# First two projection sections by turns: four accumulators fed by row blocks instead of two sections one after the other

## The chip, the cores and the metric

The kernel runs on one core of a Trainium2 chip. The core has a matrix engine (TensorE, PE in the profile), a vector engine (VectorE, DVE), an activation engine (ScalarE, ACT), GpSimd (POOL), and SyncE (SP), which here only issues DMAs; ACT issues some DMAs too. The metric is the device time of one execution in microseconds (us), as the median of several runs. The time before is 370.73 us (three runs, 370.17 to 373.01).

## The reference

One decoder layer for 256 tokens of width 1024, all in float32. What matters here is its front: the RMS norm of x, one wide input projection, and the small network that compresses keys and values.

```python
h = rmsnorm(x, norm1_g[layer])
proj = h @ w_in[layer]
q_n = proj[..., :OFF_KV]
kv_n = proj[..., OFF_KV:OFF_GN]
g_n = proj[..., OFF_GN:OFF_M]
...
k_c, v_c, k_s, v_s, k_w, v_w = (kv[:, :, i] for i in range(6))
k_s = partial_rope(k_s, cos, sin)
k_w = partial_rope(k_w, cos, sin)
kc = compress_blocks(k_c, cmp_pe_k[layer], cmp_k_w1[layer], cmp_k_w2[layer])
vc = compress_blocks(v_c, cmp_pe_v[layer], cmp_v_w1[layer], cmp_v_w2[layer])

def compress_blocks(k, pe, w1, w2):
    ...
    return jax.nn.gelu(kb @ w1) @ w2
```

Behind it come two attentions (a sparse one with 8 heads in 2 groups, and one with 8 heads), gates, an output projection, and a feed-forward part of width 4096 with a squared ReLU. The change touches only the first two sections of the projection and the steps that hang on them.

## The kernel before

**Weights in chunks.** All weights are streamed through three buffers `raw` as chunks of 128 partitions by up to 2048 numbers (`CHUNKS`, numbered from 0). Each matrix product is made exact by three products of rounded parts: `split` rounds a chunk to `whi` on ACT (L114) and leaves the rest, `wlo`, on DVE (L116); `mm3` multiplies high by high, high by low and low by high. `whi` and `wlo` have three buffers each as well, so the split of a chunk waits until PE is done with the chunk three tiles earlier, and the load of a chunk waits until the splits of the chunk three tiles earlier are done.

**The projection.** Chunks 0 and 1 are the section "kva" (384 columns: keys and values to compress, and the selected-block keys), 2 and 3 "kvb" (408 columns), 4 and 5 "q" (512), 6 and 7 "qm", and so on. The first chunk of a section holds the input rows 0 to 511 of the weights, as four row blocks of 128, the second chunk rows 512 to 1023. `xstat` makes the 24 matmul instructions of one chunk: two accumulators (token tiles t = 0, 1), four row blocks, three products. In chunks 0 and 1 the order goes by row block, with both accumulators in each, and in later chunks by accumulator. The transposed input xT arrives in parts (`x_part`), and a row block kt of it is scaled by the norm's gain and split to `hTh` (ACT, L187) and `hTl` (DVE, L193).

**Who sets the order.** Each engine executes its instructions in the order of the program text. `at(pos, f, ...)` books a step of other work into a chunk's run of matmuls, and `run_slot` emits it ahead of the matmul at that fraction of the run. So the text sets PE's order by position, and the order on ACT, DVE and SP by the sequence of the bookings. A DMA on SP or ACT that must wait for a buffer stops all that stands behind it on that engine's queue. A DMA also takes one of eight semaphore lanes in turn, and its issue waits until the DMA eight places earlier has landed.

**The steps the change moves.** `row_squares`, `row_sums`, `row_norm` compute the rows' norm (rstd). `evac_tm("kva", ...)` scales the two kva accumulators by it into `kcd` (L304) and `kva` (L307) on ACT. `cmp_gather` transposes `kcd` on PE (eight transposes, L372), `gather_evac` adds the position term into `kE` on DVE (eight adds, L384). `cmp_mlp1` is the first layer of the compressing network: 32 small matmuls of `kE` with `w1`, evacuated to `raw1` on ACT (L395), and on DVE a reduction `gsum` (L396). `cmp_sum` multiplies `raw1` by `gsum` on PE and runs the GELU; `cmp_mlp2` is the second layer. `transp_k` transposes the rotated keys. `gate_evac` puts the branch gates through a tanh on ACT (L424) and a scaling on DVE (L426).

## Time and profile before

| | |
|---|---|
| median of three runs | 370.73 us |
| the profiled execution | 371.17 us, of which its span 369.4 us |
| PE busy | 360.8 us (98%) |
| DVE, ACT busy | 311.6 us (84%), 234.2 us (63%) |
| HBM read, written | 64.87 MB, 1.05 MB |
| first matmul of the projection | starts at 4.50 us |
| first matmul of section q | starts at 25.85 us |
| first matmul of section qm | starts at 39.73 us |

All times in the rows are counted from the span's start; the profiled execution is 1.77 us longer than its span. A row of the timeline gives start, length, engine, line and operation with its tiles; the length of a matmul includes its way through the pipeline, so the distance from one start to the next tells its cost. "whi<-raw x2" are two like instructions in one row. A DMA row gives size and the time from issue to landing.

### The profile page before, as it was taken

To read this page: it belongs to the slowest core of one execution; us is meant where nothing else is said; L and a number is where in the kernel's file an instruction comes from. 1 tells how busy PE (TensorE), PEld (TensorE's weight loads), DVE (VectorE), ACT (ScalarE), POOL (GpSimd) and SP (SyncE) were. 2 spreads that over 40 slices of the span, in tenths; PEclk is the share of its full clock that TensorE was granted. 3 is DMA by queue.
4 is the path that set the end of the run, shared out by engine and by line. 5 is a ranking of instruction groups with operands and counts; after the bars stand their busy time and mean duration, and the time that the engine had idled before them with its cause. 6 is when DMAs were issued, how large, how long until landed. Compare 5 with 4: busy or idle time off the path is not lost.

```text
span 369.4 us, 5952 instructions
## 1 busy us (share of the span) xinstructions
PE 360.8 (98%) x2387; PEld 318.5 (86%) x2387; DVE 311.6 (84%) x454; ACT 234.2 (63%) x353; POOL 3.7 (1%) x15
## 2 busy tenths in 40 slices
PE   8999999999999999999999999999999999999993
PEld 6987778877778888788999999999999999999983
DVE  4988879896967769766878999999999999995875
ACT  5984364757747667525465888876766677764522
POOL 1010000000000000000000000000000000000000
PEclk9999999999999999999999999999999999999999
DMA  8987436333533334533583655444565566544003
GB/s 265 398 317 295 138 111 227 114 115 114 172 148 137 115 114 137 206 115 114 178 333 119 229 227 220 171 185 184 184 213 215 227 230 227 221 177 174 0 0 114
DMA packets 11402, 66.28 MB, mean 179 GB/s; under 512 B 1264, under 2 KB 3056, under 8 KB 4080
## 3 DMA queue, kind: packets, MB, share of 16 engines
q1 hardware_dynamic: 10512, 64.55, 47.5%
q10 hardware_dynamic: 864, 1.38, 1.1%
q8 instruction: 18, 0.29, 0.3%
q14 instruction: 8, 0.07, 0.0%
HBM read 64.87 MB, written 1.05 MB: 178 GB/s over the span
## 4 chain that ended last, share of the span: by engine, by line
PE 93%; DMA 1%; ACT 1%; issue 1%; DVE 1%; SPq 0%; POOLq 0%; POOL 0%; DVEq 0%
PE acc L238 62%; PE o L238 10%; PE yb L238 6%; PE tp L238 4%; PE qacc L238 3%; PE kvbacc L238 2%; PE Sa L238 2%; PE Sa L556 1%; DMA gx<-in_gx_dram 1%; PE tp L327 1%; PE Sb L556 1%; ACT whi L114 1%; PE Sb L238 1%; PE o L843 0%; DVE wlo L116 0%
## 5 line engine op out<-in xcount | busy, mean ns | idle before, releaser
L116 DVE TENSOR_TENSOR wlo<-raw,whi 128x1024 fp32r<-128x1024 f32 (+3 forms) x85 | 109.8, 1310 | 11.2 <-ACT whi L114 11.1
L114 ACT ACTIVATE whi<-raw 128x1024 fp32r<-128x1024 f32 (+3 forms) x84 | 93.2, 1138 | 32.1 <-PE acc L238 21.8
L238 PE MATMUL acc<-h2h,whi 128*128 128x256 f32 x256 | 70.9, 277 | 0.0
L238 PE MATMUL acc<-h2l,whi 128*128 128x256 f32 x256 | 70.7, 276 | 0.0
L238 PE MATMUL acc<-h2h,wlo 128*128 128x256 f32 x256 | 70.7, 276 | 0.0
L238 PE MATMUL acc<-whi,hTh 128*128 128x512 f32 (+1 forms) x128 | 50.7, 396 | 0.3 <-ACT whi L114 0.3
L238 PE MATMUL acc<-wlo,hTh 128*128 128x512 f32 (+1 forms) x128 | 50.5, 394 | 0.1
L238 PE MATMUL acc<-whi,hTl 128*128 128x512 f32 (+1 forms) x128 | 49.4, 386 | 0.0
L238 PEld LDWEIGHTS acc<-h2l,whi 128*128 128x128 f32 x256 | 48.1, 188 | 0.0
L238 PEld LDWEIGHTS acc<-h2h,whi 128*128 128x128 f32 x256 | 48.1, 188 | 0.0
L238 PEld LDWEIGHTS acc<-h2h,wlo 128*128 128x128 f32 x256 | 48.1, 188 | 0.0
L949 ACT ACTIVATE whi<-wt 128x2048 fp32r<-128x2048 f32 x13 | 25.0, 1921 | 25.3 <-PE acc L238 24.2
L238 PEld LDWEIGHTS acc<-whi,hTh 128*128 128x128 f32 x128 | 24.3, 190 | 6.7 <-issue 1.3
L951 DVE TENSOR_TENSOR wlo<-wt,whi 128x2048 fp32r<-128x2048 f32 x13 | 29.7, 2285 | 0.1
L238 PEld LDWEIGHTS acc<-wlo,hTh 128*128 128x128 f32 x128 | 24.2, 189 | 4.6 <-DVE wlo L116 0.7
L238 PEld LDWEIGHTS acc<-whi,hTl 128*128 128x128 f32 x128 | 24.2, 189 | 4.5
L942 DVE TENSOR_TENSOR sl<-raw,sh 128x1536 fp32r<-128x1536 f32 x13 | 22.8, 1752 | 0.0
L940 ACT ACTIVATE sh<-raw 128x1536 fp32r<-128x1536 f32 x13 | 19.4, 1489 | 3.0 <-PE acc L238 3.0
L238 PE MATMUL acc<-mxl,whi 128*128 128x256 f32 x64 | 17.8, 278 | 0.0
L238 PE MATMUL acc<-mxh,wlo 128*128 128x256 f32 x64 | 17.8, 278 | 0.0
L238 PE MATMUL acc<-mxh,whi 128*128 128x256 f32 x64 | 17.7, 276 | 0.0
L901 DVE TENSOR_TENSOR al<-aq,ah 128x896 fp32r<-128x896 f32 (+1 forms) x16 | 16.2, 1011 | 0.6 <-ACT ah L899 0.6
(279 smaller groups left out, 732.7 us busy)
## 6 DMA issues: line engine op xcount, KB each, us to landing
raw<-in_ff_dram SPq DMA_DIRECT2D x32, 1024.0 KB, 4.9
raw<-in_gm_dram SPq DMA_DIRECT2D x8, 1024.0 KB, 4.8
raw<-in_wout_dram SPq DMA_DIRECT2D x4, 1024.0 KB, 4.9
raw<-in_q_dram SPq DMA_DIRECT2D x2, 1024.0 KB, 7.1
raw<-in_qm_dram SPq DMA_DIRECT2D x2, 1024.0 KB, 6.1
raw<-in_km_dram SPq DMA_DIRECT2D x2, 1024.0 KB, 5.4
raw<-in_vm_dram SPq DMA_DIRECT2D x2, 1024.0 KB, 4.8
raw<-in_upn_dram SPq DMA_DIRECT2D x2, 1024.0 KB, 5.6
```

The source lines that it names most:

```text
L114: act.activation(hi[c][:, a:b], raw[c][:, a:b], AF.Copy)
L116: dve.tensor_tensor(lo[c][:, a:b], raw[c][:, a:b], hi[c][:, a:b].bitcast(F32), op=ALU.subtract)
L238: pe.matmul(o, l, r, start=start, stop=stop, skip_group_check=True)
L327: pe.transpose(tp[:, j * 256 + t * 128:j * 256 + t * 128 + 128], src[:, t, (2 * i + j) * 128:(2 * i + j + 1) * 128], ident)
L556: pe.transpose(T[:, j, x, o:o + 128], P[:, 2 * x + j, c:c + 128], ident)
L901: dve.tensor_tensor(A[i][2][:, 0:b - a], aq[:, a:b], A[i][1][:, 0:b - a].bitcast(F32), op=ALU.subtract)
L940: act.activation(singles[c][0], v, AF.Copy)
L942: dve.tensor_tensor(singles[c][1], v, singles[c][0].bitcast(F32), op=ALU.subtract)
L949: act.activation(hi[c], v, AF.Copy)
L951: dve.tensor_tensor(lo[c], v, hi[c].bitcast(F32), op=ALU.subtract)
```

## The change

The two sections kva and kvb are no longer computed one after the other. Their chunks are loaded in quarters by turns (0 and 2 by row block, then 1, then 3), and PE goes through the rows once: for each row block of x first six matmuls of kva, then six of kvb, in four accumulators. Chunk order of the buffers is now 0, 2, 1, 3, 4, 5. Chunk 3 is loaded by two DMAs that ACT issues. `sm` and `kc` are loaded after all quarters, and `load(5)`, `load(6)` and w1 are booked behind them at the end of the first run. The evacuations of kva (`kcd_evac` for both tiles, then `kva_evac`) come at the end of the second run; `cmp_gather` stands in chunk 4 instead of 3, `cmp_mlp1` in chunk 5 at 0.08 instead of chunk 4 at 0.7, `cmp_sum` in chunk 5 at 0.4 instead of 0.09, and `cmp_mlp2` with the second `transp_k` in chunk 6 at 0.02 instead of chunk 5 at 0.75. What is computed is the same.

```diff
--- before.py
+++ after.py
@@ -131,22 +132,26 @@
     w1 = ap_.tile([128, 2, 16, 64], F32, name="w1", tag="w1")
     xsq = ap_.tile([128, 8, 256], F32, name="xsq", tag="early")
     gx = cp.tile([128, 16 + 2048], F32, name="gx")
-    raw_tile(0)
-    raw_tile(1)
+    for c in (0, 2, 1):
+        raw_tile(c)
 
     def x_part(a, b):
         c0, c1 = (16 + 256 * a if a else 0), 16 + 256 * b
         nc.sync.dma_start(gx[:, c0:c1], gxd[:, c0:c1])
 
-    for k in range(3):
-        load_part(0, k, 4, 1, nc.scalar)
-    for a, b in ((0, 1), (1, 2), (2, 4)):
-        x_part(a, b)
-    load_part(0, 3, 4)
-    for a in (4, 6):
-        x_part(a, a + 2)
-        load_part(1, a % 4, 4, 2)
-    load(2)
+    load_part(0, 0, 4, 1, nc.scalar)
+    load_part(2, 0, 4, 1, nc.scalar)
+    load_part(0, 1, 4, 1, nc.scalar)
+    x_part(0, 1)
+    x_part(1, 2)
+    load_part(2, 1, 4)
+    for k in (2, 3):
+        x_part(k, k + 1)
+        load_part(0, k, 4)
+        load_part(2, k, 4)
+    for k in (4, 6):
+        x_part(k, k + 2)
+        load_part(1, k % 4, 4, 2)
 
     make_identity(nc, ident)
     dve.memset(mhalf, -0.5)
@@ -159,10 +164,6 @@
     pool.memset(bdk[:, 30:32], 0.0)
 
     xT = gx[:, 16:].rearrange("p (k q) -> p k q", k=8)
-    load(3)
-    nc.sync.dma_start(sm, small)
-    nc.sync.dma_start(kc_, const)
-    load(4)
     g1, g2 = gx[:, 0:8], gx[:, 8:16]
     pe_sb = sm[:, S_PE:S_PE + 32].rearrange("p (s l) -> p s l", s=2)
     w2 = sm[:, S_W2:S_W2 + 128]
@@ -183,7 +184,7 @@
 
     hTh, hTl = act_pair("hT", 16)
 
-    for kt in range(8):
+    def x_block(kt):
         act.activation(hTh[:, kt, :], xT[:, kt, :], AF.Copy, scale=g1[:, kt:kt + 1])
         if kt == 0:
             hi[0] = wp.tile([128, 2048], F32R, name="whi")
@@ -194,6 +195,12 @@
                                  hTh[:, kt, :].bitcast(F32), op0=ALU.mult, op1=ALU.subtract)
         if kt:
             split(kt // 4, kt % 4, 4)
+
+    for kt in range(4):
+        x_block(kt)
+        split(2, kt, 4)
+    nc.sync.dma_start(sm, small)
+    nc.sync.dma_start(kc_, const)
 
     stat = cp.tile([128, 8], F32, name="stat")
     rstd = cp.tile([128, 2], F32, name="rstd")
@@ -253,7 +260,7 @@
         r = []
         h, l = hi[c], lo[c]
         order = [(t, k) for t in range(2) for k in range(4)]
-        if c < 2:
+        if c < 4:
             order.sort(key=lambda e: e[1])
         for t, k in order:
             kt = kts[k]
@@ -297,13 +304,16 @@
     kcd = ap_.tile([128, 2, 4, 2, 64], F32, name="kcd")
     kvb = ap_.tile([128, 2, 408], F32, name="kvb")
     vm = ap_.tile([128, 2, 512], F32, name="vm")
-    tm = {"kva": kva, "kvb": kvb, "vm": vm}
+    tm = {"kvb": kvb, "vm": vm}
+
+    def kcd_evac(t, acc):
+        act.activation(kcd[:, t], acc[:, 0:256].rearrange("p (a d) -> p a d", a=4)[:, :, None, :]
+                       .to_broadcast([128, 4, 2, 64]), AF.Copy, scale=rstd[:, t:t + 1])
+
+    def kva_evac(t, acc):
+        act.activation(kva[:, t, :], acc[:, 256:384], AF.Copy, scale=rstd[:, t:t + 1])
 
     def evac_tm(sec, t, acc, n):
-        if sec == "kva":
-            act.activation(kcd[:, t], acc[:, 0:256].rearrange("p (a d) -> p a d", a=4)[:, :, None, :]
-                           .to_broadcast([128, 4, 2, 64]), AF.Copy, scale=rstd[:, t:t + 1])
-            acc, n = acc[:, 256:384], 128
         act.activation(tm[sec][:, t, :], acc[:, :n], AF.Copy, scale=rstd[:, t:t + 1])
 
     def rope(z, nh):
@@ -605,73 +615,82 @@
             at(0.12, d_yevac, d - 1)
 
 
-    groups = [("kva", 0, 384), ("kvb", C_KVB, 408), ("q", C_Q, 512), ("qm", C_QM, 512),
-              ("km", C_KM, 512), ("vm", C_VM, 512)]
+    first = [acc_tile(), acc_tile()]
+    second = [ps_e.tile([128, 512], F32, name=f"kvbacc{t}") for t in range(2)]
+    x_block(4)
+    raw_tile(3)
+    for k in (0, 2):
+        load_part(3, k, 4, 2, nc.scalar)
+    load(4)
+    row_squares(0)
+    row_squares(1)
+    for i in range(2):
+        a = xstat(i, 384, first, range(4 * i, 4 * i + 4))
+        if i == 0:
+            b = xstat(2, 408, second, range(4))
+
+            at(0.9, x_block, 5)
+            at(0.9, split, 3, 0, 4)
+            at(0.9, row_sums, 0, 2, 2)
+            at(0.9, split, 3, 1, 4)
+            at(0.9, row_squares, 2)
+            at(0.9, x_block, 6)
+            at(0.9, row_squares, 3)
+            for q in ((4, 6, 2), (0, 4, 2), (0, 1, 1)):
+                at(0.9, row_sums, *q)
+            at(0.9, split, 3, 2, 4)
+            at(0.9, x_block, 7)
+            at(0.9, split, 3, 3, 4)
+            at(0.95, load, 5)
+            at(0.95, load, 6)
+            at(0.95, nc.sync.dma_start, w1, w1c)
+        else:
+            b = xstat(3, 408, second, range(4, 8))
+            at(0.58, row_norm)
+            for k in range(2):
+                at(0.6, split, 4, k, 2)
+            at(0.61, load, 7)
+            for t in range(2):
+                at(0.9, kcd_evac, t, first[t])
+            for t in range(2):
+                at(0.91, kva_evac, t, first[t])
+            for k in range(2):
+                at(0.95, split, 5, k, 2, "h")
+        run_slot([m for k in range(0, 24, 6) for x in (a, b) for m in x[k:k + 6]])
+
+    groups = [("q", C_Q, 512), ("qm", C_QM, 512), ("km", C_KM, 512), ("vm", C_VM, 512)]
     for sec, c0, n in groups:
         if sec in ("q", "qm", "km"):
             tm[sec] = ap_.tile([128, 2, 512], F32, name="qtm", bufs=2)
-        if sec in ("kvb", "q"):
+        if sec == "q":
             accs = [ps_e.tile([128, 512], F32, name=f"{sec}acc{t}") for t in range(2)]
         else:
             accs = [acc_tile(), acc_tile()]
         for i in range(2):
             c = c0 + i
-            if c == 0:
-                at(0.6, load, 5)
-            elif c == 1:
-                at(0.88, row_squares, 0)
-                for k in range(4):
-                    at(0.89, split, 2, k, 4)
-                for k in range(1, 4):
-                    at(1.1, row_squares, k)
-                at(1.1, row_sums, 0, 2, 2)
-                at(1.1, row_sums, 4, 6, 2)
-                at(1.1, row_sums, 0, 4, 2)
-                at(1.1, row_sums, 0, 1, 1)
-                for k in range(4):
-                    at(1.2, split, 3, k, 4, "h")
-                for k in range(2):
-                    at(1.3, split, 3, k, 4, "l")
-
-            elif c == 2:
-                at(0.9, row_norm)
-                for k in range(2, 4):
-                    at(0.91, split, 3, k, 4, "l")
-                at(0.92, load, 6)
-                at(0.92, nc.sync.dma_start, w1, w1c)
-            elif c == 3:
-                for k in range(2):
-                    at(0.0, split, 4, k, 2, "h")
-                for t in range(2):
-                    at(0.01, evac_tm, "kva", t, first[t], 384)
-                for k in range(2):
-                    at(0.1, split, 4, k, 2, "l")
-                at(0.11, load, 7)
-                at(0.66, cmp_gather)
-                for k in range(2):
-                    at(0.66, gather_evac, k)
-                for k in range(2):
-                    at(0.7, split, 5, k, 2, "h")
-            elif c == 4:
+            if c == 4:
                 for t in range(2):
                     at(0.0, evac_tm, "kvb", t, second[t], 408)
-                at(0.1, split, 5, 0, 2, "l")
+                at(0.1, cmp_gather)
+                at(0.1, gather_evac, 0)
+                at(0.12, split, 5, 0, 2, "l")
+                at(0.13, gather_evac, 1)
                 at(0.2, rope, kva, 2)
                 at(0.3, split, 5, 1, 2, "l")
                 at(0.35, load, 8)
                 split_events(c, (0.5, 0.55), (0.8, 0.9))
-                at(0.7, cmp_mlp1)
             else:
                 std_events(c)
             unit_events(c)
             if c == 5:
                 at(0.05, gate_evac)
-                at(0.09, cmp_sum)
+                at(0.08, cmp_mlp1)
                 at(0.1, transp_k, kva, tuple(a[:, 0:1] for a in kswT))
                 at(0.1, rope, kvb[:, :, 0:128], 2)
-                at(0.75, cmp_mlp2)
-                at(0.75, transp_k, kvb[:, :, 0:128], tuple(a[:, 1:2] for a in kswT))
+                at(0.4, cmp_sum)
             if c == 6:
+                at(0.02, cmp_mlp2)
+                at(0.02, transp_k, kvb[:, :, 0:128], tuple(a[:, 1:2] for a in kswT))
                 at(0.45, transp_heads, tm["q"], qT, 0, 1)
                 at(0.6, rope, tm["q"], 8)
             if c == 7:
@@ -689,11 +708,7 @@
                 turn["tp"] = ["tp"]
                 at(0.09, transp_heads, tm["km"], kmT, 0)
                 at(0.48, transp_heads, tm["km"], kmT, 1)
-            if c == 1:
-                first = accs
-            elif c == 3:
-                second = accs
-            elif i == 1:
+            if i == 1:
                 at(0.49 if sec == "vm" else 0.5, evac_tm, sec, 0, accs[0], n)
                 at(1.0, evac_tm, sec, 1, accs[1], n)
             run_slot(xstat(c, n, accs, range(4 * i, 4 * i + 4)))```

The moved instructions at three places. First SP's queue from the program's start: the order of its DMAs. `gx` is the input x with the gains, `raw` the weight buffer of the chunk named behind the arrow. Before:

```order
L139 DMA gx<-in_gx_dram 128x512
L96 DMA raw<-in_kva_dram 128x384
L139 DMA gx<-in_gx_dram 128x512
L96 DMA raw<-in_kva_dram 128x768
L139 DMA gx<-in_gx_dram 128x512
L96 DMA raw<-in_kva_dram 128x768
L96 DMA raw<-in_kvb_dram 128x1632 x2
L163 DMA sm<-in_small_dram 128x160
L164 DMA kc<-in_const_dram 128x380
L96 DMA raw<-in_q_dram 128x2048 x2
```

And SP's queue in the changed kernel, from the fifth DMA on:

```order
L96 DMA raw<-in_kva_dram 128x384
L96 DMA raw<-in_kvb_dram 128x408
L140 DMA gx<-in_gx_dram 128x256
L96 DMA raw<-in_kva_dram 128x384
L96 DMA raw<-in_kvb_dram 128x408
L140 DMA gx<-in_gx_dram 128x512
L96 DMA raw<-in_kva_dram 128x768
L140 DMA gx<-in_gx_dram 128x512
L96 DMA raw<-in_kva_dram 128x768
L202 DMA sm<-in_small_dram 128x160
L203 DMA kc<-in_const_dram 128x380
L96 DMA raw<-in_q_dram 128x2048 x2
```

The first kvb chunk moved forward, in quarters between those of x and kva. The second kvb chunk is gone from this queue. In both kernels the two q chunks follow kc; the second of them needs the buffer of chunk 2 before and of chunk 1 now.

The second place is ACT in chunks 4 and 5, where the evacuation of the first layer (`raw_78`, the tile raw1) and the tanh of the gates stand among the splits of chunks 6 and 7 (128x1024 each). Before:

```order
L307 ACTIVATE kvb<-kvbacc_275,rstd 128x408
L114 ACTIVATE whi<-raw 128x1024 x2
L395 ACTIVATE raw_78<-tp 128x64
L114 ACTIVATE whi<-raw 128x1024
L424 ACTIVATE gates<-kvb 128x12x2 x2
L403 ACTIVATE gl<-tp 128x30
```

And in the changed kernel:

```order
L317 ACTIVATE kvb<-kvbacc_191,rstd 128x408
L114 ACTIVATE whi<-raw 128x1024 x3
L434 ACTIVATE gates<-kvb 128x12x2 x2
L405 ACTIVATE raw_78<-tp 128x64
L355 ACTIVATE kswh<-tp 128x256
L413 ACTIVATE gl<-tp 128x30
```

The evacuation of raw1 moved behind the third split, which is the first half of chunk 7, and behind the gates.

The third place is DVE in the same stretch: `gsum` feeds cmp_sum on PE, and the gates' scaling needs ACT's tanh. Before:

```order
L320 TENSOR_TENSOR kva<-ropa,ropb 128x2x16
L116 TENSOR_TENSOR wlo<-raw,whi 128x1024
L396 TENSOR_REDUCE gsum<-ident 128x32
L116 TENSOR_TENSOR wlo<-raw,whi 128x1024 x2
L426 TENSOR_SCALAR gates<-gates 128x48
L404 TENSOR_TENSOR gl<-gl 128x30
```

And in the changed kernel:

```order
L330 TENSOR_TENSOR kva<-ropa,ropb 128x2x16
L116 TENSOR_TENSOR wlo<-raw,whi 128x1024 x3
L436 TENSOR_SCALAR gates<-gates 128x48
L406 TENSOR_REDUCE gsum<-ident 128x32
L356 TENSOR_TENSOR kswl<-tp,kswh 128x256
L327 TENSOR_TENSOR ropa<-kvb,kc 128x32
```

The reduction gsum moved behind both halves of chunk 6 and behind the gates' scaling.

## The prediction

> **What bounds the kernel now.** First the page and the list of waits of PE, the engine that is nearly always busy:
>
> ```profile
> PE 360.8 (98%) x2387; PEld 318.5 (86%) x2387; DVE 311.6 (84%) x454; ACT 234.2 (63%) x353; POOL 3.7 (1%) x15
> PE tp L372 <- ACT kcd L304: 0.5, 1, 0.5
> PE acc L238 <- ACT whi L114: 0.3, 1, 0.3
> ```
>
> PE has two waits of its own inside the projection, 0.8 us together, so little can be gained at all. What they cost in full is seen in PE's timeline, from start to start:
>
> ```profile
> 4.50 0.66 PE L238 MATMUL acc<-whi,hTh 128*128 128x384 f32 x1
> ...
> 7.30 0.34 PE L238 MATMUL acc<-whi,hTl 128*128 128x384 f32 x1
> 7.99 0.44 PE L238 MATMUL acc<-whi,hTh 128*128 128x384 f32 x1 [0.34 <-ACT whi L114]
> 8.58 0.45 PE L238 MATMUL acc<-wlo,hTh 128*128 128x384 f32 x1
> ...
> 14.59 0.33 PE L238 MATMUL acc<-whi,hTl 128*128 128x384 f32 x1
> ...
> 22.70 0.33 PE L372 MATMUL tp<-ident,kcd 128*128 128x128 f32 x1
> 23.54 0.98 PE L372 MATMUL tp<-ident,kcd 128*128 128x128 f32 x7 [0.50 <-ACT kcd L304]
> ...
> 31.65 0.40 PE L238 MATMUL qacc<-whi,hTl 128*128 128x512 f32 x1
> ...
> 33.02 0.39 PE L238 MATMUL qacc<-whi,hTl 128*128 128x512 f32 x1
> 33.34 0.30 PE L238 MATMUL tp<-gsum,raw 64*64 64x30 f32 x4
> 33.57 0.44 PE L354 MATMUL tp<-ident,kva 128*128 128x128 f32 x2
> ```
>
> From 8.58 to 14.59 there are 34 steps, 0.18 us each. From 7.30 to 8.58 there are two, so the third row block cost 0.9 us of waiting for x and its split. The first transpose of kcd stands 0.84 us ahead of the second where a step of a few tenths would do: some 0.6 us. Behind these PE has no wait in the list up to the end of the projection. So the change can win at most 0.9 + 0.6 = 1.5 us there, perhaps half a microsecond more in the first six matmuls after 4.50. The bound against it is all that must arrive and be split by the time PE wants it.
>
> **The change part by part.** The same matmuls, splits, evacuations and bytes are executed, so PE's own time is unchanged and only waits differ. I follow them to one mark, the matmuls of cmp_sum, which start at 33.34 before. In the changed order PE has by then done seven more matmuls of q (six steps in 33.02 - 31.65 = 1.37, so 0.23 each, 1.6) and the two transposes of kva (0.4). At equal work the mark of before is therefore 33.34 + 2.0 = 35.3.
>
> *When the second kvb chunk arrives.* Rows of the DMA issues, one issue each, with SP's times of issue behind them:
>
> ```profile
> raw<-in_kva_dram ACTq DMA_DIRECT2D x1, 192.0 KB, 3.2
> raw<-in_kva_dram SPq DMA_DIRECT2D x1, 384.0 KB, 5.9
> raw<-in_kvb_dram SPq DMA_DIRECT2D x1, 816.0 KB, 7.2
> raw<-in_kvb_dram SPq DMA_DIRECT2D x1, 816.0 KB, 5.3
> raw<-in_qm_dram SPq DMA_DIRECT2D x1, 1024.0 KB, 4.7
> raw<-in_qm_dram SPq DMA_DIRECT2D x1, 1024.0 KB, 7.4
> 4.84 0.65 SPq L96 DMA_DIRECT2D raw<-in_kva_dram  x1
> 5.53 4.22 SPq L96 DMA_DIRECT2D raw<-in_kvb_dram  x2
> 12.88 2.81 SPq L96 DMA_DIRECT2D raw<-in_q_dram  x2
> 20.57 0.33 SPq L96 DMA_DIRECT2D raw<-in_qm_dram  x1
> 23.55 0.33 SPq L96 DMA_DIRECT2D raw<-in_qm_dram  x1
> ```
>
> Before, the last piece of kva landed at 4.84 + 5.9 = 10.7, with 1992 KB asked for on SP, and the first kvb chunk at 5.53 + 7.2 = 12.7, with 2808 KB. In the new order SP has asked for 2156 KB by the first half of chunk 1, so this lands at about 10.7 + 2.0 x 164 / 816 = 11.1. ACT splits its first quarter and only then issues the two DMAs of chunk 3, at about 11.5: in ACT's order they stand behind that split. The first half (408 KB) then takes at least the 3.2 of the first row (192 KB on an empty queue) and at most the 5.3 of the fourth (816 KB behind others): it lands at L = 14.7 to 16.8. I take 14.7, since ACT's queue is empty then as in the first row.
>
> Against that choice: SP's load of the first q chunk runs at the same time. The fourth row, 816 KB with others on their way, took 0.6 longer than the fifth, 1024 KB alone. The Trainium skill, DMA: Bandwidth & Descriptors, section Issuing engines are not separate DMA queues, says that DMAs started by different engines end on the same 16 DMA engines and interleave there; the rows of this case point the same way. By that rule the half chunk would get half of the rate, and at the 2.8 us per 1024 KB worked out below it would come 1.1 us later, which would make the sum below 1.1 us longer. It is inside the bounds of L.
>
> PE wants the half chunk at 4.50 plus one pass of 48 matmuls at 0.18 plus six, and the first waits: about 15. Nothing is lost or won here beyond a few tenths.
>
> *From there DVE is a chain.* Rows of DVE, then of ACT:
>
> ```profile
> 10.17 0.48 DVE L193 SCALAR_TENSOR_TENSOR hTl<-gx,hTh 128x256 fp32r<-128x256 f32 x1
> 10.57 0.56 DVE L116 TENSOR_TENSOR wlo<-raw,whi 128x384 fp32r<-128x384 f32 x1
> 11.04 0.48 DVE L193 SCALAR_TENSOR_TENSOR hTl<-gx,hTh 128x256 fp32r<-128x256 f32 x1
> 13.28 2.06 DVE L116 TENSOR_TENSOR wlo<-raw,whi 128x408 fp32r<-128x408 f32 x4 [0.42 <-ACT whi L114]
> 15.26 0.68 DVE L207 TENSOR_TENSOR xsq<-xsq 128x512 f32<-128x512 f32 x1
> 16.15 1.88 DVE L207 TENSOR_TENSOR xsq<-xsq 128x512 f32<-128x512 f32 x3 [0.20 <-ACT xsq L204]
> 21.16 2.36 DVE L116 TENSOR_TENSOR wlo<-raw,whi 128x1024 fp32r<-128x1024 f32 x2 [0.62 <-ACT whi L114]
> 30.52 0.37 DVE L396 TENSOR_REDUCE gsum<-ident 128x32 f32<-128x128 f32 x1
> 32.77 1.06 ACT L114 ACTIVATE whi<-raw 128x1024 fp32r<-128x1024 f32 x1 [1.56 <-PE qacc L238]
> 33.73 0.32 ACT L424 ACTIVATE gates<-kvb 128x24 f32<-128x24 f32 x2
> ```
>
> Behind the arrival of chunk 3 there is ACT's split (0.5) and then, in DVE's order up to the last quarter of chunk 1, three wlo of 408 (0.52 each), four sums (0.68 + 1.88) and twice hTl with wlo of 384 (0.87 from 10.17 to 11.04): 5.8. Only then is the buffer of chunk 1 free, and SP can issue the load of the second q chunk: at L + 6.3 = 21.0. Before, that load was the second of the two at 12.88, issued at 15.4; it has moved by 5.6 us, and queued behind it on SP are the load of chunk 6, w1 and the load of chunk 7. The latter needs the two wlo of chunk 4 (0.5 + 0.1 + 2.4 later, L + 9.3).
>
> Before, three such loads ran in a row from 20.57: the first landed at 25.3 (4.7), the third at 23.55 + 7.4 = 31.0, so 2.8 us for each more. Now there are four: the last, chunk 7, lands 4.7 + 3 x 2.8 = 13.2 after the first issue, at L + 19.5 = 34.2, where it landed at 31.0.
>
> *Who waits for chunk 7.* On ACT its first half stands ahead of the gates' tanh and of raw1's evacuation, and on DVE the gates' scaling stands ahead of gsum; cmp_sum on PE waits for raw1 and gsum, and behind it all matmuls are queued. From the split's start to the end of gsum it is 33.73 - 32.77 + 0.32 + about 0.2 for the scaling + 0.4 = 1.9. So cmp_sum starts at 34.2 + 1.9 = 36.1, and 36.1 - 35.3 = 0.8 us later than before at equal work. w1, which lands 2.8 us ahead of chunk 7, is wanted by PE about 3 us ahead of cmp_sum; what PE waits for it lies inside the same wait.
>
> The rest I cost at nothing. The kcd transposes now stand behind six kvb and three q matmuls, and the evacuations they need take less; without that cover they cost the 0.6 of before. cmp_mlp2 has 14 matmuls (14 x 0.23 = 3.2) between it and cmp_sum. The ACT queue's two issues hold ACT for under 1 us, hidden while PE has a row block in hand.
>
> **The sum.** On the profiled execution's own time 371.17 + 0.8 = 372.0. This execution was 0.4 above the median of the runs, 370.73, so the forecast is 370.73 + 0.8 = 371.5. From the bounds: L at its upper end gives + 2.9; L cannot act before 13 (chunk 3's rounded parts go into the buffers of chunk 0, which PE frees at the end of the first pass), which gives - 0.9.
>
> **The rivals.** (A) *The gain is kept.* The loads land sooner than reckoned, or PE finds the late steps ready: then the waits of 0.9 and 0.6 are gone, less a wait for the second quarter of kva, now third on ACT's queue, of 0 to 0.9. For it: PE has a pass and a half of matmuls to hide the loads, and if each of the four loads took half a microsecond less, 2 us would go from the chain. Against it: three loads in a row did take 2.8 each. With 0.2 for that wait the time is 370.73 - 1.3 = 369.4, at best 368.7.
>
> (B) *Chunk 3 comes late.* Its two DMAs run beside the first q chunk (1024 KB), which SP issues about then. If its first half took the 7.2 of the third row, L would be 18.7, and the same chain gives 0.8 + 4.0 = 4.8, so 375.5. It decides from 14.7 + 2.9 = 17.6 on: there the sum passes 3.7 us, which is 1%. For it: 7.2 was measured with much queued ahead. Against it: the load asks for half as much, on a queue with nothing ahead.
>
> (C) *The start does not change:* the wait moves from the third row block to the second, since a third DMA on ACT is late again. That alone gives 370.7, and under my forecast it changes nothing, because the chain through chunk 7 ends last in any case.
>
> **How the numbers follow.** Changes under 1% (3.7 us) are what a measurement of this kernel can hardly tell from none. My forecast with its bounds has 0.56, A 0.26, B 0.08, C 0.08; 0.02 is for something else. More than 1% faster would need more than all waits named here together, 0.02. Slower by over 1% is B and a little of the forecast's upper end, 0.10. The rest, 0.88, lies within 1%. The range runs from 368.8, near A's best, to the forecast's upper end, 370.73 + 2.9 = 373.6.
>
> **What would show it.** Right: SP issues the second q chunk near 21; PE waits about 2 us at the small matmuls of w1 and cmp_sum, named after a DMA, ACT or DVE; the waits at 7.99 and 23.54 are gone or smaller; section qm starts no earlier than before at equal work. Wrong: that issue before 18, or no wait of PE between 25 and 40 us (then A); a wait of PE over 2 us near 15, named after the split of chunk 3 (then B).

## The result and the profile after

The changed kernel takes 375.91 us (median of six runs, 375.49 to 377.76), the kernel before 370.42 in the same comparison: a ratio of 1.0145, with a 95% interval of 1.0118 to 1.0172. The forecast was 371.5 with a range up to 373.6; rival B had given 375.5. The profiled execution after took 375.59, its span is 373.8, against 371.17 and 369.4 before.

The row of busy times in the profile of the changed kernel (below called after), and then PE's waits (engine, line, for whom: total, times, longest):

```profile
PE 362.1 (97%) x2387; PEld 319.7 (86%) x2387; DVE 311.4 (83%) x454; ACT 234.2 (63%) x353; POOL 4.7 (1%) x15
...
PE kvbacc L245 <- ACT whi L114: 3.5, 1, 3.5
...
PE tp L245 <- DVE gsum L406: 0.4, 1, 0.4
PE acc L245 <- DVE wlo L116: 0.2, 1, 0.2
```

The work is the same; PE is busy 1.3 us longer. Both waits of before are gone from the list; one of 3.5 us has come, with two small ones of 0.4 and 0.2. PE's timeline shows its place and what follows it (start, length, engine, line, operation; the distance between starts is the cost):

```profile
15.03 0.34 PE L245 MATMUL acc<-whi,hTl 128*128 128x384 f32 x1
18.83 0.71 PE L245 MATMUL kvbacc<-whi,hTh 128*128 128x408 f32 x1 [3.47 <-ACT whi L114]
19.45 0.71 PE L245 MATMUL kvbacc<-wlo,hTh 128*128 128x408 f32 x1
...
20.30 0.54 PE L245 MATMUL kvbacc<-whi,hTh 128*128 128x408 f32 x1
20.64 0.54 PE L245 MATMUL kvbacc<-wlo,hTh 128*128 128x408 f32 x1
...
22.27 0.34 PE L245 MATMUL acc<-whi,hTh 128*128 128x384 f32 x1
22.45 0.34 PE L245 MATMUL acc<-wlo,hTh 128*128 128x384 f32 x1
...
39.45 0.30 PE L245 MATMUL tp<-gsum,raw 64*64 64x30 f32 x4 [0.43 <-DVE gsum L406]
```

Six matmuls into the second run PE stops before chunk 3. When it goes on, its steps take 0.34 us where they took 0.18, until 22.27: nine steps in 3.44 us, 1.8 more than nine at 0.18. Some 0.5 of this is the wait for DVE's half of the split behind the restart, which the runs at full clock show too; 1.3 is a slower clock. The granted clock says why (windows of 1 us; behind the bracketed counts stand the clock, the share of the DMA engines and GB/s):

```profile
18.00:19.00 1.00, 0.17 (x1) 0.17 (x1) 0.19 (x1) 0.76 (x2) 0.00 (x0) 0.92 0.10 39
19.00:20.00 1.00, 1.00 (x3) 0.66 (x4) 1.00 (x3) 1.00 (x3) 0.00 (x0) 0.50 0.00 0
21.00:22.00 1.00, 1.00 (x5) 0.99 (x4) 0.97 (x3) 1.00 (x4) 0.00 (x0) 0.50 0.00 0
23.00:24.00 1.00, 1.00 (x7) 1.00 (x6) 1.00 (x4) 1.00 (x2) 0.00 (x0) 1.00 0.00 0
```

What PE waited for stands in the timelines of ACT and SP, with two rows of the DMA issues (KB, us from issue to landing) at the end, those of chunk 3's first half and of chunk 7:

```profile
11.93 0.53 ACT L114 ACTIVATE whi<-raw 128x384 fp32r<-128x384 f32 x1 [0.84 <-DMA raw<-in_kva_dram]
11.94 0.82 ACTq L96 DMA_DIRECT2D raw<-in_kvb_dram  x2
18.24 0.98 ACT L114 ACTIVATE whi<-raw 128x408 fp32r<-128x408 f32 x2 [3.47 <-DMA raw<-in_kvb_dram]
...
10.94 13.92 SPq L96 DMA_DIRECT2D raw<-in_q_dram  x2
27.63 0.33 SPq L96 DMA_DIRECT2D raw<-in_qm_dram  x1
...
raw<-in_kvb_dram ACTq DMA_DIRECT2D x1, 408.0 KB, 6.2
raw<-in_qm_dram SPq DMA_DIRECT2D x1, 1024.0 KB, 9.7
```

ACT issued chunk 3 at 11.94 and its first half landed 6.2 later, at L = 18.2. From there the loads came as the prediction's chain has it: the second q chunk was issued at 10.94 + 13.92 less the issue itself, near 24.5 (L + 6.3), chunk 7 landed at 27.63 + 9.7 = 37.3 (L + 19.1, reckoned 19.5), cmp_sum started at 39.45 (L + 21.2, reckoned 21.4).

Why 6.2: the queues' rows for 11 to 15, 15 to 16, 16 to 17 and 17 to 18 us (packets, MB, share of the 16 engines' time; q1 is SP's queue, q10 ACT's).

```profile
q1 hardware_dynamic: 601, 1.56, 103.2%
q1 hardware_dynamic: 39, 0.25, 60.3%
q10 hardware_dynamic: 35, 0.11, 32.5%
q10 hardware_dynamic: 120, 0.36, 89.5%
q1 hardware_dynamic: 13, 0.04, 10.1%
q10 hardware_dynamic: 114, 0.32, 79.4%
```

Up to 15 us ACT's queue moved nothing: SP's, with the last of kva, x, the constants and the q load that had been asked for a microsecond ahead of chunk 3, held all 16 engines. Then both halves of chunk 3 came together, not one behind the other: of their 0.84 MB, 0.79 had moved by 18.0, when the first half was just short of complete. A queue with nothing ahead in it was no empty road.

### The profile page after: what moved, and what is told of

Same layout as the page of the kernel before. It is cut to its first block, busy times and chain, and to the rows that moved or that the text cites. A ratio compares the mean times of both kernels' runs of the same rounds, so it can differ in the third digit from the quotient of the medians.

```text
span 373.8 us, 5958 instructions
## 1 busy us (share of the span) xinstructions
PE 362.1 (97%) x2387; PEld 319.7 (86%) x2387; DVE 311.4 (83%) x454; ACT 234.2 (63%) x353; POOL 4.7 (1%) x15
## 4 chain that ended last, share of the span: by engine, by line
PE 89%; DMA 4%; DVE 3%; issue 2%; ACT 0%; SPq 0%; POOLq 0%; POOL 0%; DVEq 0%; ACTq 0%
PE acc L245 61%; PE o L245 10%; PE yb L245 6%; PE tp L245 4%; DMA raw<-in_kvb_dram 3%; PE kvbacc L245 2%; PE Sa L245 2%; PE Sa L566 1%; DMA raw<-in_kva_dram 1%; DVE wlo L116 1%; PE qacc L245 1%; PE tp L337 1%; PE Sb L566 1%; DVE kE L394 1%; PE Sb L245 1%
## 5 line engine op out<-in xcount | busy, mean ns | idle before, releaser
L116 DVE TENSOR_TENSOR wlo<-raw,whi 128x1024 fp32r<-128x1024 f32 (+3 forms) x85 | 109.7, 1309 | 15.5 <-ACT whi L114 15.4
L114 ACT ACTIVATE whi<-raw 128x1024 fp32r<-128x1024 f32 (+3 forms) x84 | 93.3, 1137 | 37.8 <-PE acc L245 21.9
L245 PE MATMUL acc<-h2h,whi 128*128 128x256 f32 x256 | 71.0, 277 | 0.0
L245 PE MATMUL acc<-h2l,whi 128*128 128x256 f32 x256 | 70.8, 277 | 0.0
L245 PE MATMUL acc<-h2h,wlo 128*128 128x256 f32 x256 | 70.8, 276 | 0.0
L245 PE MATMUL acc<-whi,hTh 128*128 128x512 f32 (+1 forms) x128 | 51.0, 398 | 0.0
L245 PE MATMUL acc<-wlo,hTh 128*128 128x512 f32 (+1 forms) x128 | 50.8, 397 | 0.2 <-DVE wlo L116 0.2
L245 PE MATMUL acc<-whi,hTl 128*128 128x512 f32 (+1 forms) x128 | 49.4, 386 | 0.0
L245 PEld LDWEIGHTS acc<-h2l,whi 128*128 128x128 f32 x256 | 48.1, 188 | 0.0
L245 PEld LDWEIGHTS acc<-h2h,whi 128*128 128x128 f32 x256 | 48.1, 188 | 0.0
L245 PEld LDWEIGHTS acc<-h2h,wlo 128*128 128x128 f32 x256 | 48.1, 188 | 0.0
L245 PEld LDWEIGHTS acc<-whi,hTh 128*128 128x128 f32 x128 | 24.4, 191 | 6.1 <-issue 1.3
L245 PEld LDWEIGHTS acc<-wlo,hTh 128*128 128x128 f32 x128 | 24.3, 190 | 4.6 <-DVE wlo L116 0.6
L245 PEld LDWEIGHTS acc<-whi,hTl 128*128 128x128 f32 x128 | 24.2, 189 | 4.5
L245 PE MATMUL acc<-mxl,whi 128*128 128x256 f32 x64 | 17.8, 278 | 0.0
L245 PE MATMUL acc<-mxh,wlo 128*128 128x256 f32 x64 | 17.8, 278 | 0.0
L245 PE MATMUL acc<-mxh,whi 128*128 128x256 f32 x64 | 17.7, 277 | 0.0
## 6 DMA issues: line engine op xcount, KB each, us to landing
raw<-in_ff_dram SPq DMA_DIRECT2D x32, 1024.0 KB, 5.0
raw<-in_gm_dram SPq DMA_DIRECT2D x8, 1024.0 KB, 4.8
raw<-in_wout_dram SPq DMA_DIRECT2D x4, 1024.0 KB, 4.8
raw<-in_q_dram SPq DMA_DIRECT2D x2, 1024.0 KB, 5.5
raw<-in_qm_dram SPq DMA_DIRECT2D x2, 1024.0 KB, 8.3
raw<-in_km_dram SPq DMA_DIRECT2D x2, 1024.0 KB, 5.2
raw<-in_vm_dram SPq DMA_DIRECT2D x2, 1024.0 KB, 4.8
raw<-in_upn_dram SPq DMA_DIRECT2D x2, 1024.0 KB, 4.8
```

Source lines behind the costliest of these rows:

```text
L114: act.activation(hi[c][:, a:b], raw[c][:, a:b], AF.Copy)
L116: dve.tensor_tensor(lo[c][:, a:b], raw[c][:, a:b], hi[c][:, a:b].bitcast(F32), op=ALU.subtract)
L245: pe.matmul(o, l, r, start=start, stop=stop, skip_group_check=True)
```

## The experiments

In all of them the measure is "copy", the time at which ACT copies cmp_sum's result (39.79 after; 33.95 before, with less work ahead of it), and L, at which ACT's first copy of chunk 3 starts. Theory 1, the load chain: what hangs on chunk 3's landing has a fixed length, and the end moves with L. Theory 2, PE: its wait and the half clock are what costs, and the chain runs beside them.

**Chunk 3 on SP, ahead of the q load** (e1_c3_on_sp):

```diff
     for k in (0, 2):
-        load_part(3, k, 4, 2, nc.scalar)
+        load_part(3, k, 4, 2)
     load(4)
```

> The changed kernel with chunk 3's two DMAs issued by SP, ahead of the first q chunk, instead of by ACT beside it. Load-chain theory (the half chunk came late because it shared the DMA engines with the q chunk, and the end is set by the chain from that arrival over DVE to the load of chunk 7 and gsum, 21.3 us after the arrival): the half lands near 15.2 instead of 18.2, PE's wait of 3.5 shrinks below 1, cmp_sum starts at 36.5 instead of 39.45, and the time is 375.9 - 2.9 = 373.0. PE theory (only PE's wait and the low clock behind it count): both go, 3.6 + 1.8 us, and the time is 370.6.

374.27 us, ratio 1.0094 (1.0071 to 1.0116): above what either theory had given (373.0 and 370.6), and nearer to theory 1. L is 15.6 and the copy at 37.0, L + 21.5 as in after (18.2 and 39.8, L + 21.6); the clock stays at 1.00. PE's wait is down to 0.7:

```profile
PE kvbacc L245 <- ACT whi L114: 0.7, 1, 0.7
PE tp L382 <- ACT kcd L310: 0.6, 2, 0.3
PE tp L245 <- DVE gsum L406: 0.6, 1, 0.6
```

So 2.8 of PE's wait and all of the half clock (1.3) are gone, 4.1 together, and the copy came 2.8 earlier, about as much as L (2.7): new waits for kcd and gsum have taken the rest. That speaks for theory 1. The span is only 1.4 shorter than that of after; a later stretch, which ran 1.1 longer in this trace, is treated at the end.

**The q load behind chunk 3 on ACT's queue** (e2_q_behind_c3):

```diff
         load_part(3, k, 4, 2, nc.scalar)
-    load(4)
+    raw_tile(4)
+    load_part(4, 0, 1, 1, nc.scalar)
```

> The changed kernel with the first q chunk issued by ACT behind chunk 3 instead of by SP beside it; chunk 3 is issued when it was. If sharing with the q chunk is why the half chunk took 6.2 us: it takes about 3.5 and lands near 15.4, and the time is that of the run with chunk 3 on SP plus 0.2, about 373.2 (load-chain theory) or 370.9 (PE theory). If it is slow by itself, because ACT issues it late and a DMA then takes that long: 6 us as before and 375.9.

374.46 us, ratio 1.0102 (1.0073 to 1.0131), between the two. L is 17.4, 0.8 earlier, and the copy at 39.2, L + 21.8. Without the q load ahead, chunk 3's first half still took 5.4 and landed at 17.3: what SP had asked for before (the last of kva, x and the constants) was under way until 13. Nor did the q load stay behind: ACT's queue moved 1.38 MB by 17.0, and chunk 3 is 0.84 of it, so at least 0.54 MB of the q load had gone beside chunk 3 before its first half was complete. The run shows that the q load ahead is a part of the lateness; how large a part it can't show, since the load still ran beside.

**PE kept at full clock** (e3_warm_pe): 32 transposes of the identity, which nothing reads, stand before chunk 3's first matmul.

```diff
+        mms = [m for k in range(0, 24, 6) for x in (a, b) for m in x[k:k + 6]]
+        if i == 1:
+            mms[6] = (lambda f: lambda: ([pe.transpose(warm[:, 0:128], ident, ident)
+                                          for _ in range(32)], f()))(mms[6])
+        run_slot(mms)
-        run_slot([m for k in range(0, 24, 6) for x in (a, b) for m in x[k:k + 6]])
```

> The changed kernel with 32 extra transposes of the identity on PE in its 3.5 us wait ahead of chunk 3's first matmul; they feed nothing. The granted clock should stay near 1.0 from 18.8 to 22.3 us where it was 0.5. PE theory: PE keeps 1.5 to 1.8 us, 374.2. Load-chain theory: cmp_sum still waits for gsum and starts at 39.4, its wait grows from 0.4 to about 2, and the time stays 375.9.

377.02 us, ratio 1.0167 (1.0145 to 1.0189): not better. The granted clock is 1.00 throughout, steps behind the wait take 0.18 again, and yet:

```profile
14.85 3.66 PE L661 MATMUL yb<-ident 128*128 128x128 f32 x32
...
PE tp L245 <- DVE gsum L406: 0.9, 1, 0.9
PE kvbacc L245 <- ACT whi L114: 0.8, 1, 0.8
PE tp L382 <- ACT kcd L310: 0.6, 2, 0.3
```

PE is sooner at kcd and gsum and waits there instead (0.9 for gsum, where 2 had been expected). L was 18.7 in this trace, 0.5 later than in after, and the copy at 40.5, L + 21.8. The half clock in after cost nothing that could be had back by itself. Theory 2 falls.

**The later steps alone, on the kernel before** (e4_later_steps):

```diff
+                for t in range(2):
+                    at(0.9, kcd_evac, t, first[t])
+                for t in range(2):
+                    at(0.91, kva_evac, t, first[t])
...
-                at(0.7, cmp_mlp1)
+                at(0.08, cmp_mlp1)
-                at(0.09, cmp_sum)
+                at(0.4, cmp_sum)
```

> The kernel before with the second part of the change alone: keys' evictions, transposes and the small network's layers later, the two sections still one after the other. Load-chain theory: chunk 7 lands at 31.0 as before, so gsum is there by 33 and nothing waits; the wait at the kcd transposes goes, 0.6: 370.4 - 0.6 = 369.8. If the later places cost by themselves: PE waits at cmp_sum or cmp_mlp2 and the time is 370.4 or more.

371.37 us, ratio 1.0004 (0.9988 to 1.0019): no difference. The 369.8 that theory 1 had expected did not come. The wait for kcd is gone from the trace and that for x's third row block from the list of waits (from start to start the block still costs 0.5: 7.04 to 7.90 for two steps); a wait for gsum (0.5) is there. So the loss of the change does not lie in the moved steps, but in the sections by turns.

**Chunk 3 issued just ahead of the q load** (e5_c3_issued_earlier):

```diff
-    x_block(4)
     raw_tile(3)
     for k in (0, 2):
         load_part(3, k, 4, 2, nc.scalar)
+    x_block(4)
     load(4)
```

> After, with ACT issuing chunk 3's two loads ahead of the fifth row block's copies, so about 1 us earlier (near 10.95 instead of 11.94) and at the same moment as SP issues the first q load (10.94). In after's trace ACT's queue moved no byte before 15 us, while SP's queue held all 16 engines with the q load, and chunk 3's first half landed at 18.2. If the q load was merely first, by a microsecond, chunk 3 now shares the engines with it: L is 16 to 17, and the time follows L one for one, 373.9 to 374.9. If SP's queue is served ahead whatever the order of issue, L stays near 18.2 and the time at 375.9.

375.89 us, ratio 1.0146 (1.0117 to 1.0176): the time of after. Now ACT's two DMAs were asked for at 10.18, half a microsecond ahead of the q load, and the queues' rows for 11 to 15 us show both at work:

```profile
q1 hardware_dynamic: 492, 1.12, 74.0%
q10 hardware_dynamic: 162, 0.48, 30.3%
```

So the engines are shared, and SP's queue isn't served first whatever the order. But shared means slow: the first half took 6.9 and landed at 17.2, only 1.0 earlier for an issue 1.8 earlier. The copy came at 39.1 (L + 21.9), 0.7 earlier. The 373.9 to 374.9 expected did not come; whether the time followed by the copy's 0.7, four runs (375.22 to 377.81) can't tell.

**The kernel before once more** (e6_before_again), for its trace.

> The kernel before, unchanged, for its trace on the same chip as the other runs of this call. In the four experiments so far the matmuls of 256 columns in the stretch from about 178 us on go at a pace of 118 ns each, where the traces of before and after show 113 ns, and that stretch is 1.1 us longer in all four, whatever the edit. If that belongs to the chip, this trace shows 118 ns too and a span near 370.0; if it belongs to the edits, it shows 113 ns and 369.4.

One run, 371.36, span 369.4 as in the first trace. But cmp_sum starts at 32.29 where it was 33.34. Of the two waits on which rival A rested, that for kcd is not there (the eight transposes follow each other from 22.44 on). The third row block is not in the list of waits either, yet from start to start it still costs 0.7 (7.30 to 8.36 for two steps) where the first trace has 0.9. A stretch from about 178 us on is 1.1 longer; it is treated at the end. The pace of that stretch is not the edits', since this kernel shows it too.

**Chunk 3 ahead of the q load and of the constants** (e7_c3_first), and the same with the chain cut (e6_c3_first_chain_cut):

```diff
-    nc.sync.dma_start(sm, small)
-    nc.sync.dma_start(kc_, const)
+    raw_tile(3)
+    for k in (0, 2):
+        load_part(3, k, 4, 2)
...
     load(4)
+    nc.sync.dma_start(sm, small)
+    nc.sync.dma_start(kc_, const)
```

The cut, in the second of them:

```diff
+        if c == 5:
+            split_events(c, (0.09, 0.45), (0.3, 0.46))
...
     row_squares(1)
+    dve.tensor_reduce(gsum, ident.rearrange("p (g i) -> p i g", g=4), op=ALU.add, axis=AX)
...
         act.activation(raw1, tp[:, 0:64], AF.Copy)
-        dve.tensor_reduce(gsum, ident.rearrange("p (g i) -> p i g", g=4), op=ALU.add, axis=AX)
```

> After, with chunk 3's two loads issued by SP right behind chunk 1's, ahead of the first q load and of the two small constants (270 KB), which go behind the q load. All theories: chunk 3's first half lands at L = 15.55 (with the constants ahead of it) less 270 KB at 390 GB/s, 0.7, so 14.9, where my prediction had 14.7. Load-chain theory: the four runs so far have cmp_sum's copy on ACT at L + 21.5 to 21.8, so here at 36.5, 3.3 before after's 39.8: time 372.7. PE theory (what PE executes and waits for sets the end, the chain is beside it): waits for chunk 3 of 3.6 and 1.7 of half clock go, and 0.3 of the wait for gsum stay: cmp_sum's copy at 34.6, time 370.8.

> The same, and in addition cmp_sum no longer stands behind chunk 7's load: gsum (a sum of the identity) is formed while DVE waits for chunk 3, and the gates and raw1 come before chunk 7's copy on ACT. Load-chain theory: the chain ends at chunk 7, which PE needs 3.5 us after cmp_sum, so PE alone is left: cmp_sum's copy on ACT at 34.6 to 35.2, 0.4 to 1.0 earlier than before's at equal work (35.6), time 369.4 to 370.0 against 370.4, or 0.4 to 1.0 below before on its own chip. If instead cmp_sum waits for something else at the same place, it stays at the time of the run without the cut.

Without the cut 372.90 us, ratio 1.005 (1.0029 to 1.0071), near theory 1's 372.7. L is 14.9, near the prediction's 14.7; the copy came at 37.4, L + 22.5, and not at 36.5, since w1 and chunk 7 took longer than in the runs above (chunk 7 11.0 from issue to landing, there 9.7 to 10.3; PE waits 0.4 for w1 and 1.1 for gsum). With the cut 372.71, ratio 1.0044 (1.0027 to 1.0060): the copy came at 36.1 in the trace, L + 20.8, but I had expected 0.4 to 1.0 less than before, and it is 1.9 more. PE's waits there:

```profile
PE tp L385 <- ACT kcd L313: 0.6, 2, 0.3
PE kvbacc L246 <- ACT whi L114: 0.6, 1, 0.6
PE kvbacc L246 <- DVE wlo L116: 0.2, 1, 0.2
```

Two things were wrong in it. The base: I had reckoned from the first trace of before, and in the second one cmp_sum stands 1.05 earlier. And the turns: PE reaches chunk 3 at 15.1, L was 15.3 in this trace, the splits come on top, and ACT's copies into kcd start at L + 9.7. So even an early landing finds PE, ACT and DVE standing before chunk 3 with nothing in hand. That place in the order, at which chunk 3 must be there, is called the gate below; the next but one experiment moves it.

**The cut and the full clock together** (e9_chain_cut_warm): e3's transposes with the cut, chunk 3 as late as in after.

> After, with the chain cut in the same way (gsum early, gates and raw1 before chunk 7's copy) and with the 32 identity transposes that keep TensorE at full clock over its wait for chunk 3; L stays at 18.2 to 18.7. With the transposes alone the time was 377.0. Load-chain theory: half clock was hidden behind the chain there, and now that the chain no longer ends in cmp_sum, PE's time counts: 0.9 (the wait for gsum in that run) off, 376.1. If the half clock had cost its 1.7 us all along, 374.2.

376.19 us, ratio 1.0143 (1.0111 to 1.0174), as theory 1 had it (376.1), not 374.2. The wait for gsum is gone, the copy came at 40.0 with L at 19.2: L + 20.8 instead of 21.8. L was 0.5 later than with the transposes alone, so the agreement to a tenth is in part luck. The waits for kcd (0.6) stay. What the half clock costs once the chain is cut, without the transposes, was not run.

**The turns in the first run only** (e11_second_run_sections). The second run does chunk 1 first, while chunk 3 is on its way, and ACT and DVE form row blocks 5 to 7 and a square ahead of chunk 3's copies:

```diff
-        run_slot([m for k in range(0, 24, 6) for x in (a, b) for m in x[k:k + 6]])
+        run_slot([m for k in range(0, 24, 6) for x in (a, b) for m in x[k:k + 6]] if i == 0 else a + b)
...
+            for kt in (5, 6, 7):
+                at(0.9, x_block, kt)
+            at(0.9, row_sums, 0, 2, 2)
+            at(0.9, row_squares, 2)
+            at(0.9, split, 3, 0, 4)
...
-            at(0.58, row_norm)
+            at(0.74, row_norm)
```

And the same with chunk 3 ahead of the q load and the chain cut, as above (e12_sections_c3_first).

> After, with the turns kept in the first run only: the second run does all of chunk 1 (24 matmuls, 4.2 us) and then all of chunk 3. ACT and DVE form row blocks 5 to 7 and the squares in the time in which they waited for chunk 3, ahead of its copies. Chunk 3's loads stay on ACT's queue behind the q load. If what cost the time is that six matmuls after the start of the second run PE, ACT and DVE all stood before chunk 3, PE now reaches chunk 3 at 15.2 + 3.1 = 18.3 and finds it a microsecond late at most; the last matmul of the second section starts near 23.8 instead of 28.5, where before has 24.6 to 25.7, and the time is 370.0 to 371.0. If the load chain behind chunk 3's landing sets the end wherever PE is, the time stays near 375.9.

> The same, and chunk 3's loads on SP ahead of the first q load and of the constants (L near 15.2), and cmp_sum freed of chunk 7's load. PE then waits for nothing up to cmp_sum: the last matmul of the second section near 23.4, time 369.5 to 370.2; against the run without these two edits the gain is only what is left there of the waits for chunk 3 and gsum, 0.5 to 1.0.

With chunk 3 as late as ever: 373.55 us, ratio 1.0073 (1.0052 to 1.0095), 2.4 less than after. Chunk 3's first half landed at 13.19 + 6.1 = 19.3, later still, since chunk 1's own first quarter came at 13.18 in this trace (11.93 in after); and PE lost 0.3 us to it, and 0.4 at the next step:

```profile
19.58 0.34 PE L245 MATMUL acc<-whi,hTl 128*128 128x384 f32 x1
20.01 0.46 PE L245 MATMUL kvbacc<-whi,hTh 128*128 128x408 f32 x1
...
PE tp L245 <- DVE gsum L406: 1.0, 1, 1.0
PE acc L245 <- ACT whi L114: 0.5, 1, 0.5
PE tp L245 <- DMA w<-in_w_dram: 0.3, 1, 0.3
```

The copy is at 38.2, L + 18.8 instead of L + 21.6. The run moves PE's order and that of ACT and DVE at once; which of the two won the time, it doesn't separate. The time is not the 370 to 371 expected: the late landing of that trace (the wait of 0.5 is for chunk 1) and the loads behind it (w1 0.3, gsum 1.0) are left. With these two treated as well, 370.29 us, ratio 0.9990 (0.9975 to 1.0005): 3.3 less than without them, where 0.5 to 1.0 had been expected. From chunk 3 to cmp_sum PE waits for nothing, but it still does at the start:

```profile
7.52 0.44 PE L246 MATMUL acc<-whi,hTh 128*128 128x384 f32 x1 [0.25 <-ACT whi L114]
8.11 0.44 PE L246 MATMUL acc<-wlo,hTh 128*128 128x384 f32 x1 [0.16 <-DVE wlo L116]
...
18.51 0.33 PE L246 MATMUL acc<-whi,hTl 128*128 128x384 f32 x1
18.69 0.34 PE L246 MATMUL kvbacc<-whi,hTh 128*128 128x408 f32 x1
...
34.11 0.30 PE L246 MATMUL tp<-gsum,raw 64*64 64x30 f32 x4
```

The whole loss is accounted for by what these runs change together: the late landing of chunk 3, the gate, and the chain through chunk 7. And no gain is shown: kcd is waited for no longer, but the wait at the start has moved to the second row block of kva and costs 0.8 in this trace (6.92 to 8.11 for two steps), nearly as much as the third row block did before (0.9 and 0.7 in its two traces).

**The later steps with the chain cut, on before** (e10_later_chain_cut): the earlier run of the later steps, with the cut.

> Before's sections one after the other with the later steps of the change alone, and with cmp_sum freed of chunk 7's load (gsum formed at the start, the gates and raw1 ahead of chunk 7's copy). In the run of the later steps alone PE waited 0.5 for gsum, and for nothing else in that stretch. If that was all that held them back, 0.5 less than that run: 370.5 where before is 371.0, a difference that is at the edge of what can be measured. If the later steps only move work about, the same as before.

370.14 us, ratio 0.9987 (0.9973 to 1.0001). The wait for gsum is gone and the size is the one expected (0.6 against before's 370.73), but the interval still holds 1. It is the fastest of all, and not shown to be faster than before.

## Why the prediction was wrong

**What failed is one term, L, in "When the second kvb chunk arrives".** I put the half chunk at 3.2 us, the row of a load on an empty machine, "since ACT's queue is empty then", and its upper bound at 5.3; it took 6.2, issued 0.4 later than reckoned. L was 18.2, not 14.7, and above the upper bound of 16.8 as well. The sum with the measured L is 0.8 + 3.5 = 4.3 at cmp_sum; measured is 39.45 - 35.3 = 4.15, and the span grew by 4.4. So L is 3.5 of the 4.4 us by which the forecast was short (375.91 against 371.5). The other 0.9 is about what the base differs by: against the second trace of before, cmp_sum came 39.45 - 34.3 = 5.15 later, near the 5.5 by which the medians differ. That this is the reason isn't shown. The row that answered the question was quoted: 384 KB on busy engines took 5.9. I bounded by the size of one half and by its own queue, where the full queue was the other one and both halves came together. Chunk 3 on SP, ahead of the q load, shows it from the other side: with L at 15.6 the half took 5.1.

**What PE waits for** came out the other way round. The prediction has PE lose at most a few tenths at chunk 3 and wait about 2 us at w1 and cmp_sum; it waited 3.5 at chunk 3 and 0.4 at gsum. The chain through chunk 7 did end last, but by these 0.4 alone.

**Right:** the chain behind L, step by step (L + 6.3, L + 19.1, L + 21.2), and that it ends in cmp_sum's wait for gsum; of the traces with neither the cut nor another order in the second run, five with L from 15.6 to 18.7 have the copy at L + 21.5 to 21.9, and the sixth, with slower loads behind chunk 3, at L + 22.5. Cutting the chain took about a microsecond more off (L + 20.8). Rival B named the mechanism, the point from which it decides (17.6) and nearly the time (375.5); its 0.08 was the error. That its time is so near is in part luck: it rests on L = 18.7, and with the 18.2 measured its sum gives 370.73 + 4.3 = 375.0. The sign named for it, "a wait of PE over 2 us near 15", came true word for word.

**The rule that was weighed.** The Trainium skill, DMA: Bandwidth & Descriptors, section Issuing engines are not separate DMA queues, says that DMAs of different engines interleave on the same 16; taking equal shares, which is my reading and not in that section, I reckoned L 1.1 later. The sharing is seen where both queues are asked at the same time (0.48 and 1.12 MB in 11 to 15 us with chunk 3 issued first); in after, where the q load and much else had been asked for a little earlier, ACT's queue got nothing for 3 us, and the delay was 3.5. The rule pointed the right way, and I took the other value; equal shares would have been too little as well.

**Left out:** the half clock behind a long wait. It cost PE 1.3 us and the kernel, by the run with transposes, nothing, because kcd and gsum are no earlier.

**Rival A's ground.** The 1.5 us which the change could win were read from one execution. In a second trace of the same kernel the wait for kcd is not there and the third row block costs 0.7, so the ground was less than half as large, and the two versions without the gate's wait (0.9990 and, on before, 0.9987) show no gain that could be told from none.

**Rival C** was right about the start: the wait moved from the third row block to the second. In after ACT waits 0.85 for the second quarter of kva, the third DMA on its queue, and PE loses 0.5 there (7.17 to 8.04 for two steps):

```profile
7.17 0.43 PE L245 MATMUL acc<-whi,hTh 128*128 128x384 f32 x1
7.76 0.45 PE L245 MATMUL acc<-wlo,hTh 128*128 128x384 f32 x1 [0.15 <-DVE wlo L116]
```

It decided nothing in after, because it lies ahead of the gate, where PE waits 3.5 in any case. In the trace of the version without that wait (e12_sections_c3_first) it takes back what the start could have gained.

**Changes under 1%**, which the prediction held to be hardly told from none, were told here: the ratio 1.005 of the run with chunk 3 first has an interval from 1.0029 to 1.0071.

## What to carry to other kernels

In these runs a load's landing was set by what else was on the shared DMA engines, in whatever queue it stood: bytes asked for a microsecond earlier held it back whole, bytes asked for just after it ran beside it. Price it by the row of a small load on a busy machine, not by its own queue. Before two weight streams are worked off by turns, ask which matmuls would still be ready if the later stream were 3 us late; putting those, and the splits that can go first, ahead of the gate won 2.4 us here with the load as late as before. And where PE, ACT and DVE all hang on one landing, as in the order by turns, the end was that landing plus a nearly fixed length, so the spread of the forecast is the spread of the landing.

## What the runs showed of the hardware

**The clock also fell after a wait of 2.7 us, and late.** After a distance of 3.0 us between two matmuls (14.75 to 17.79, a wait of 2.7) in the run with chunk 3 issued just ahead of the q load, PE went on at full clock until about 19.5 (0.73 in that window) and only then fell to half, for 3.4 us:

```profile
18.00:19.00 1.00, 0.83 (x4) 0.59 (x4) 1.00 (x3) 1.00 (x4) 0.00 (x0) 1.00 0.02 7
19.00:20.00 1.00, 1.00 (x6) 1.00 (x5) 1.00 (x3) 1.00 (x4) 0.00 (x0) 0.73 0.00 0
21.00:22.00 1.00, 1.00 (x5) 0.98 (x5) 0.96 (x2) 1.00 (x3) 0.00 (x0) 0.50 0.00 0
```

In after (3.8 between starts) it fell at once and was back 3.4 later. The Trainium skill, TensorE: Matmul & The Clock Gate, section What's actually happening, has half clock after an idle window of about 3.4 us and full clock after a busy one of that length. The return agrees; that a distance of 3.0 sufficed, with the fall later, does not follow from that sentence.

**A later stretch has two paces.** In the 30 us from about 178 us on, matmuls of 256 columns follow each other at 113 ns in some traces and at 118 in others; as groups of that stretch, in the first trace of before and in the second:

```profile
L238 PE MATMUL acc<-mxl,whi 128*128 128x256 f32 x50 | 13.8, 276 | 0.0
...
L238 PE MATMUL acc<-mxl,whi 128*128 128x256 f32 x50 | 14.1, 281 | 0.0
```

That is 1.1 us for the stretch, at a granted clock of 1.00 in both. Both paces were seen on the same chip (118 in the second trace of before, 113 with chunk 3 first), and for the same kernel, so neither the chip nor the edit decides it; what does is open. Together with the start, which differs by as much between the two traces of before, it is why one trace was a poor base for a gain of 1 us.
